# An encoder layer with two attention groups: the first modulation in half blocks, products of V ahead of the first unit, rope tables among the fillers, and denser steps of the second modulation

## The chip, the cores and the metric

The kernel runs on one core of one Trainium2 chip. The metric is device time in microseconds (us) of one execution, the median of several runs. A core has five instruction streams: TensorE (PE, with its weight loads as PEld), VectorE (DVE), ScalarE (ACT), GpSimd (POOL) and SyncE (SP), which here issues the DMAs. Each engine works through its own stream in order; semaphores tie the streams together.

## The reference, cut to what matters

One layer on a sequence of 1024 tokens of width 1024, all in float32. A conditioning vector c gives six vectors of 1024 (shift, scale and gate for the mixer and for the channel part):

```
mod = silu(c) @ w_ada + b_ada                    # w_ada: 1024 x 6144
sh_a, sc_a, g_a, sh_m, sc_m, g_m = split(mod, 6)
h    = rmsnorm(x, g_attn_norm) * (1 + sc_a) + sh_a
proj = h @ w_in                                  # q_lat, kv_lat, k_rope, ca_qkv
q, k, v of 8 latent heads: up-projections of the latents, rmsnorm, rope(q, positions), rope(k, positions)
o_mla = chunk-causal attention(q, k, v)          # 8 heads
cq, ck = rmsnorm per head of ca_qkv; cv
o_ca  = attention over a band of 9 chunks of 64, with relative bias     # 8 heads
x = x + g_a * (concat(o_mla, o_ca) @ w_out)
h = rmsnorm(x, g_mlp_norm) * (1 + sc_m) + sh_m
u = causal_dwconv(h @ w_up, width 3); x = x + g_m * ((silu(gate) * val) @ w_down)
```

rope needs sin and cos of position times frequency, for 1024 positions and 16 frequencies.

## The kernel before, in words

Products that need float32 are done as three products of a high and a low part (`gemm3`). Weights come as 256-column pieces (`load_w`: a DMA on SP, the high part on ScalarE, the low part on GpSimd).

**The start.** SP loads the packed vectors, the eight tiles of x (128 tokens by 1024, 512 KB each), the first 1 MB block of the modulation's weights (`adaw_0`), and the weights `wq0`. Each tile of x is squared and summed on ScalarE (line 212), its root on GpSimd (`rsqrt_mean`, line 116, an operation of power), and scaled on VectorE (line 214). Then a loop goes over the eight blocks d of 128 columns. In each block VectorE multiplies eight pieces of `adaw_d`, 256 wide (128 columns of scale and 128 of shift), by the conditioning vector's eight columns and adds them up (`adacc`, lines 241 and 243); two small matmuls (`p_ada`) sum over the partitions; VectorE makes the block's column of `modT` (lines 249 to 251). `mod_transpose` turns x into columns (four transposes on TensorE), applies `modT` twice on ScalarE (`hT`, the high part, line 224, and `hv`) and takes the low part on VectorE or GpSimd. 24 products with `wq0` follow (line 150), which build q and k of the first pair of heads for all 1024 tokens in PSUM (`qk0`).

Behind the loop `rope_tables` computes the sin and cos tables on VectorE (two Sin on ScalarE). Then `qk_norm` normalises q and k of the first pair: copy and square on ScalarE, a reduce on VectorE, the power and the multiply (line 373) on GpSimd. The buffers of the start are given back to the attention's pool at that place.

**The attention.** It consists of 32 units (16 of banded heads, 16 of latent heads; `ca_unit`, `mla_unit`), each of four tiles of 128 queries. `prep` transposes q and k to pages (`qk_page`, line 615). `Unit.scores` issues the products of scores (line 655), the minimum on VectorE (lines 670 and 674; the scores are negated), Exp on ScalarE (line 681), the high and low half-precision parts of the probabilities, and a transposing DMA on SP. `Unit.values`, three tiles later, multiplies by V (line 721).

**The fillers.** Between the tiles the program puts pieces of other work, from a list of generators: `v0` (`f_v(0)`, the products of V for the first two pairs, 192 matmuls in PSUM tiles `ipv0`), `qk1`, `qk2` (tiles `ipq`), `v1`, `qk3`, `m` (the latents, `f_m`, which need the rope tables), `up0`, `up1`, `oca`. `pace` issues as many pieces as a ratio of the costs of the scores and values asks for; `need` issues all pieces of the keys that a unit needs. Most filler keys also feed a side generator `f_ada`, which computes the gate of the mixer and the second modulation: per step two DMAs of 128 KB and two multiply-adds 256 wide on VectorE (`aacc`, lines 428 and 430), or a small matmul. One step is taken for every 2000 ns of filler cost; there are 73 steps.

```
            if key not in ("v0", "up0", "up1", "oca"):
                nside[0] += c
                while nside[0] > 2000:
                    nside[0] -= 2000
                    next(side[0], None)
```

**What sets the order.** A scheduler orders the instructions of each engine from the program by its own simulation of the times, within the dependences, with raised priority for scores, probabilities and values (`tc.high_priority`). `tc.issue_after(x)` holds an instruction behind instruction x in its engine's order. Buffers come from tagged pools: a tile waits until the tile that last had its buffer is done. Tag "A" (three buffers of 256) serves `adacc`, `aacc` and the pieces `aw`; tag "pg" has six buffers.

Behind the attention come the output projection and the MLP (from `load_wo(0, ...)` on), with a third modulation piece `gmbc` (lines 1008 and 1010, the same kind of multiply-add, 512 wide).

Of the kernel before, what the change touches and what calls it, by code (L numbers as in the profile page):

```python
# [23 lines left out]
P = 128  # L24
D = 1024
# [12 lines left out]
GSTEP, LAG = 2, 4  # L38
DEPTH = 3
# [19 lines left out]
def _grid(x, q):  # L59
    return round(x / q) * q  # L60


def layer_kernel(ctx, tc, I, out):
# [81 lines left out]

    def gemm3(pt, pairs, start=True, stop=True):

        n = len(pairs)
        for i, (sh, sl, mh, ml) in enumerate(pairs):
            pe.matmul(pt, sh, mh, start=(start and i == 0), stop=False)  # L150
            pe.matmul(pt, sh, ml, start=False, stop=False)  # L151
            pe.matmul(pt, sl, mh, start=False, stop=(stop and i == n - 1))  # L152
# [17 lines left out]
    def load_w(name, src, ncol, he="a", ssw=None):  # L170
        tiles = []
        for k in range(ND):
# [7 lines left out]
            for c0 in range(0, ncol, 256):  # L180
# [4 lines left out]
                if ssw is not None:  # L185
                    junk = qtile(f"{name}j{k}")
# [6 lines left out]

    xs = []
# [6 lines left out]
    wada = []  # L201

    def load_ada(d):
        w = st.tile([P, ND, 2, P], F32, name=f"adaw_{d}", tag="wa", bufs=2)
        sp.dma_start(w[:], I["w_ada_a"][d])
        wada.append(w)

    load_ada(0)
# [26 lines left out]
    qk0 = [ps.tile([P, 1024], F32, name=f"qk0_{i}", tag="S", bufs=2) for i in range(2)]  # L235
    for d in range(ND):
        if d + 1 < ND:
            load_ada(d + 1)
        w = wada[d]
        acc = apg.tile([P, 2, P], F32, name=f"adacc_{d}", tag="A", bufs=3)  # L240
        dve.tensor_scalar(acc[:], w[:, 0], cs[:, 0:1], None, op0=MUL)
        for k in range(1, ND):
            dve.scalar_tensor_tensor(acc[:], w[:, k], cs[:, k:k + 1], acc[:], op0=MUL, op1=ADD)
        pt = ps.tile([P, 512], F32, name=f"p_ada{d}", tag="mm", bufs=2)
        for i in range(2):
            pe.matmul(pt[:, i:i + 1], acc[:, i, :], ones[:, 0:1], start=True, stop=True)
# [15 lines left out]
    def rope_tables():  # L262
        sp.dma_start(pos_i[:], I["pos"])
        buf = [st.tile([P, 8, NT, 16], F32, name=f"rt{i}", tag="x", bufs=4) for i in range(8)]
        cnt = [0]

        def T():
            cnt[0] += 1
            return buf[(cnt[0] - 1) // 8][:, (cnt[0] - 1) % 8]

        def rnd(src, q):
            o = T()
            dve.tensor_scalar(o, src, q, MAGIC, op0=MUL, op1=ADD)
            dve.tensor_scalar(o, o, MAGIC, None, op0=SUB)
            return o

        def fma(n, c, b):
            o = T()
            dve.scalar_tensor_tensor(o, n, c, b, op0=MUL, op1=ADD)
            return o  # L280

        p1 = _grid(TWO_PI, 2.0 ** -9)
        p2 = _grid(TWO_PI - p1, 2.0 ** -21)
        p3 = TWO_PI - p1 - p2

        def reduce(src):
            n = rnd(src, 1.0 / TWO_PI)
            r = fma(n, -p1, src)
            r = fma(n, -p2, r)
            return fma(n, -p3, r)  # L290

        pf = cst.tile([P, NT], F32, name="pf")
        dve.tensor_copy(pf[:], pos_i[:])
        ang = T()
        dve.tensor_tensor(ang, pf[:].unsqueeze(2).to_broadcast([P, NT, 16]),
                          pk[:, C_INV:C_INV + 16].unsqueeze(1).to_broadcast([P, NT, 16]), op=MUL)
        nh = rnd(ang, 2.0 ** -20)
        rem = fma(nh, -(2.0 ** 20), ang)
        nm = rnd(rem, 2.0 ** -8)
        lo = fma(nm, -(2.0 ** 8), rem)  # L300
        tot = reduce(lo)
        for n, w in ((nh, 2.0 ** 20), (nm, 2.0 ** 8)):
            c = w - round(w / TWO_PI) * TWO_PI
            c1 = _grid(c, 2.0 ** -9)
            x = T()
# [1053 lines left out]
```

## Time and profile before

| | before |
|---|---|
| median of 3 runs | 1423.73 us (1421.95 to 1424.95) |
| profiled execution | 1423.74 us, of it 1422.0 us of span |
| mean granted TensorE clock | 0.936 |
| TensorE busy | 1247.1 us (88%), 6704 matmuls |
| VectorE busy | 1081.8 us (76%) |
| GpSimd busy | 686.6 us (48%) |
| ScalarE busy | 620.6 us (44%) |
| DMA | 190.64 MB, mean 134 GB/s |

How to read it: the span goes from the first to the last recorded instruction. Shares are of the span. A row of an engine in "busy tenths" cuts the span into 40 equal slices of 35.55 us and gives the busy share of each in tenths; PEclk is the clock granted to TensorE in tenths of full speed. A row of a group has line, engine, operation, output <- inputs, shapes and count, then total busy us and mean ns of one, then the engine's idle time just before them and what ended most of it. A row of the timeline begins with the start in us and the duration; behind it stands in brackets the wait ahead of it and what ended it. A row of the table of stretches has the stretch, its length, the busy us of the engines with their counts, the granted clock, the DMA share and GB/s.

### The profile page before, as it was taken

How to read it: one execution, taken by the hardware profiler on the slowest of the kernel's cores; microseconds unless marked ns; L12 is line 12 of the kernel's file. 1: busy time of each engine (PE TensorE's matmuls, PEld its weight loads, DVE VectorE, ACT ScalarE, POOL GpSimd, SP SyncE). 2: the span in 40 equal slices, each digit the busy share in tenths (PEclk: the TensorE clock that was granted, in tenths of full speed). 3: DMA queues.
4: the chain of work that ended last, by engine and by line, in shares of the span. 5: the costliest groups of instructions: out<-in, count | busy, mean ns of one | idle time of the engine just before them, and what ended most of it. 6: DMA issues, size and time to landing. Idle time of an engine off the chain costs nothing.

```text
span 1422.0 us, 19886 instructions
## 1 busy us (share of the span) xinstructions
PE 1247.1 (88%) x6704; PEld 1031.6 (73%) x6704; DVE 1081.8 (76%) x1891; ACT 620.6 (44%) x1150; POOL 686.6 (48%) x673
## 2 busy tenths in 40 slices
PE   3859989998877688886695999999999999999998
PEld 2759977987765567765574887877778777888886
DVE  6864877566689997684467789989888889688667
ACT  4453344334356554453255443343344443543331
POOL 5263545265555673334562675676667775200000
PEclk9979996999888889997896999999999999999999
DMA  8423557545441478778731233333323223894451
GB/s 289 134 74 79 119 111 146 139 107 119 104 94 41 88 163 159 161 148 224 275 126 30 90 111 126 125 122 116 111 84 102 97 96 112 309 356 126 126 163 59
DMA packets 229602, 190.64 MB, mean 134 GB/s; under 512 B 149366, under 2 KB 180218, under 8 KB 228476
## 3 DMA queue, kind: packets, MB, share of 16 engines
q1 hardware_dynamic: 229500, 189.38, 48.1%
q8 instruction: 52, 0.85, 0.2%
q14 instruction: 50, 0.41, 0.1%
HBM read 117.24 MB, written 37.49 MB: 109 GB/s over the span
## 4 chain that ended last, share of the span: by engine, by line
PE 20%; DVE 19%; POOL 5%; issue 5%; ACT 4%; DMA 3%; SPq 1%; DVEq 0%; POOLq 0%; ACTq 0%
DVE u L1024 5%; DVE u L1023 4%; PE dnA_P L1171 2%; PE dnA_P L1173 2%; PE dnA_P L1172 2%; ACT u L1022 2%; PE dnB_P L1173 1%; PE dnB_P L1171 1%; PE dnB_P L1172 1%; DVE gmbc L1010 1%; DVE u L1100 1%; DVE c L1095 1%; DMA adaw<-w_ada 1%; PE p L934 1%; PE p L932 1%
## 5 line engine op out<-in xcount | busy, mean ns | idle before, releaser
L75 ACT ACTIVATE dnP<-dnr 128x1024 fp32r<-128x1024 f32 x73 | 77.4, 1062 | 111.0 <-PE dnA_P L1173 46.4
L1145 DVE TENSOR_TENSOR dnP<-dnr,dnP 128x1024 fp32r<-128x1024 f32 x72 | 88.3, 1230 | 47.0 <-ACT dnP L75 46.4
L1023 DVE SCALAR_TENSOR_TENSOR u<-c,pk,u 128x1023 f32<-128x1023 f32 x44 | 81.8, 1901 | 46.2 <-ACT u L1022 44.8
L71 POOL TENSOR_SCALAR hlm<-Pm,rim 128x512 f16<-128x512 f32 (+3 forms) x96 | 67.2, 710 | 79.6 <-DVE rim L684 36.0
L1024 DVE SCALAR_TENSOR_TENSOR u<-c,pk,u 128x1022 f32<-128x1022 f32 x44 | 84.3, 1955 | 0.0
L71 POOL TENSOR_SCALAR hlc<-Pc,ric 128x640 f16<-128x640 f32 (+2 forms) x64 | 45.3, 710 | 78.8 <-DVE ric L684 31.5
L681 ACT ACTIVATE Pc<-sc,mc 128x640 f32<-128x640 f32 (+2 forms) x64 | 42.1, 659 | 85.9 <-DVE mc L670 64.3
L655 PE MATMUL sm<-mk,mq 96*128 96x512 f32 (+3 forms) x288 | 70.1, 372 | 10.2 <-ACT Pm L681 6.8
L430 DVE SCALAR_TENSOR_TENSOR aacc<-aw,cs,aacc 128x256 f32<-128x256 f32 x84 | 44.5, 529 | 43.1 <-DMA aw<-w_ada 42.4
L655 PE MATMUL sc<-k,q 64*128 64x512 f32 (+3 forms) x288 | 70.6, 374 | 6.4 <-ACT Pc L681 3.8
L721 PE MATMUL pvm<-PTm,vt 128*128 128x128 f16 x576 | 48.2, 235 | 30.0 <-DMA PTm<-hlm 25.7
L705 DVE SCALAR_TENSOR_TENSOR hlm<-Pm,rim,hlm 128x512 f16<-128x512 f32 (+3 forms) x96 | 68.3, 725 | 5.2 <-POOL hlm L71 4.9
L721 PEld LDWEIGHTS <-vt 128*128 128x128 f16 x576 | 39.6, 106 | 40.7 <-issue 38.9
L681 ACT ACTIVATE Pm<-sm,mm 128x128 f32<-128x128 f32 (+3 forms) x64 | 47.2, 737 | 46.6 <-DVE mm L674 23.1
L655 PEld LDWEIGHTS sm<-mk,mq 96*128 96x128 f32 x288 | 49.7, 200 | 19.9 <-ACT Pm L681 10.1
L655 PEld LDWEIGHTS sc<-k,q 64*128 64x128 f32 x288 | 48.1, 209 | 20.3 <-ACT Pc L681 5.2
L1022 ACT ACTIVATE u<-c,pk 128x1024 f32<-128x1024 f32 x44 | 52.2, 1234 | 16.7 <-DVE c L1095 9.3
L75 ACT ACTIVATE wc<-ws 128x512 fp32r<-128x512 f32 x22 | 13.9, 632 | 102.9 <-DVE ws L949 102.9
L150 PE MATMUL ipq<-wq_s,hT 128*128 128x256 f32 x192 | 57.2, 298 | 0.0
L705 DVE SCALAR_TENSOR_TENSOR hlc<-Pc,ric,hlc 128x640 f16<-128x640 f32 (+2 forms) x64 | 48.9, 769 | 9.3 <-POOL hlc L71 9.2
L151 PE MATMUL ipq<-wq_s,hT 128*128 128x256 f32 x192 | 55.8, 291 | 0.0
L152 PE MATMUL ipq<-wq_s,hT 128*128 128x256 f32 x192 | 55.0, 287 | 0.0
(404 smaller groups left out, 4464.9 us busy)
## 6 DMA issues: line engine op xcount, KB each, us to landing
wu<-w_up SPq DMA_DIRECT2D x44, 512.0 KB, 3.5
dnr<-g_d SPq DMA_DIRECT2D x73, 256.0 KB, 4.2
aw<-w_ada SPq DMA_DIRECT2D x96, 128.0 KB, 2.3
g_d<-u SPq DMA_DIRECT2D x22, 512.0 KB, 2.7
dnr<-w_down SPq DMA_DIRECT2D x44, 256.0 KB, 5.4
x<-x SPq DMA_DIRECT2D x16, 512.0 KB, 8.4
adaw<-w_ada_a SPq DMA_DIRECT2D x8, 1024.0 KB, 5.1
g_d<-gs SPq DMA_DIRECT2D x22, 256.0 KB, 2.1
```

Of the source, the lines that this page charges most:

```text
L71: pool.tensor_scalar(o, i, s, 1.0, op0=MUL, op1=MUL)
L75: act.activation(o, i, AF.Copy)
L150: pe.matmul(pt, sh, mh, start=(start and i == 0), stop=False)
L151: pe.matmul(pt, sh, ml, start=False, stop=False)
L655: last = pe.matmul(s[:, c:c + w], qpg[rs_, a, q], kpgs[kh][rs_, b, ko:ko + w], start=(a == 0 and b == 0), stop=(a == 1))
L681: act.activation(pr[:, :n], sv, AF.Exp, bias=m[:], scale=-1.0, accum_out=rsum[:, 0:1])
L705: dve.scalar_tensor_tensor(hl[:, w:2 * w], pp, ri[:], hl[:, :w], op0=MUL, op1=SUB)
L721: last = pe.matmul(u.pv[:, c], u.vst(j), mov, start=(x == 0), stop=(x == len(todo) - 1))
L1022: act.activation(u[:], c, AF.Identity, scale=pk[:, cv + 2:cv + 3], bias=pk[:, cv + 3:cv + 4])
L1023: dve.scalar_tensor_tensor(u[:, 1:], c[:, :S - 1], pk[:, cv + 1:cv + 2], u[:, 1:], op0=MUL, op1=ADD)
L1024: dve.scalar_tensor_tensor(u[:, 2:], c[:, :S - 2], pk[:, cv:cv + 1], u[:, 2:], op0=MUL, op1=ADD)
L1145: r = f(*a, **k)
```

## The change

- **First modulation in half blocks.** The weights are laid out on the host as four pairs of blocks, each `[128, 8, 512]`. A pair is loaded in four pieces of `[128, 2, 512]` (512 KB, tag "wa", five buffers in place of two of 1 MB). The four pieces of pair 0 are loaded ahead of x, and the positions ahead of them. VectorE makes one accumulator per pair with eight multiply-adds 512 wide (32 in all, where there were 64 of 256); pair dd+1 is issued at the first block of pair dd.
- **Products of V ahead of unit 0.** The weights `wv0` are loaded inside the loop at block 4, and 16 filler steps (`NPRE`) are issued before the first unit. The scale of V (`pow2_scale`) is issued behind the first tile's products instead of ahead of them. The transposes of `qk_page` are held behind the last of these products.
- **Normalisation of the first pair.** The multiply of `qk_norm` for `qk0` goes to VectorE.
- **Rope tables among the fillers.** `rope_tables` becomes a generator with 14 rotating and two kept slots in two "pg" tiles; it takes a step at each filler step of `qk1`, held behind the last minimum of the scores on VectorE. What is left of it is issued at the start of `f_m`. The two Sin stand next to each other in the program.
- **Denser second modulation.** One step per 1500 ns of filler. Its loads are held behind the last transposing DMA on SP, its multiply-adds behind the last minimum on VectorE.

```diff
+NPRE = 16
...
     def gemm3(pt, pairs, start=True, stop=True):
...
-            pe.matmul(pt, sl, mh, start=False, stop=(stop and i == n - 1))
+            last = pe.matmul(pt, sl, mh, start=False, stop=(stop and i == n - 1))
+        anchor["pe"] = last.ins
...
+    sp.dma_start(pos_i[:], I["pos"])
+    def load_ada(dd, c):
+        w = st.tile([P, 2, 512], F32, name=f"adaw_{dd}_{c}", tag="wa", bufs=5)
+        sp.dma_start(w[:], I["w_ada_a"][dd][:, 2 * c:2 * c + 2])
+        wada[dd, c] = w
+    for c in range(4):
+        load_ada(0, c)
     xs = []
...
+    def ada_pair(dd):
+        acc = rtile(f"adacc_{dd}")
+        for k in range(ND):
+            w = wada[dd, k // 2][:, k % 2]
+            if k == 0:
+                dve.tensor_scalar(acc[:], w, cs[:, 0:1], None, op0=MUL)
+            else:
+                dve.scalar_tensor_tensor(acc[:], w, cs[:, k:k + 1], acc[:], op0=MUL, op1=ADD)
+        accs[dd] = acc
+    ada_pair(0)
     for d in range(ND):
-        if d + 1 < ND:
-            load_ada(d + 1)
-        w = wada[d]
-        acc = apg.tile([P, 2, P], F32, name=f"adacc_{d}", tag="A", bufs=3)
-        dve.tensor_scalar(acc[:], w[:, 0], cs[:, 0:1], None, op0=MUL)
-        for k in range(1, ND):
-            dve.scalar_tensor_tensor(acc[:], w[:, k], cs[:, k:k + 1], acc[:], op0=MUL, op1=ADD)
+        dd, half = divmod(d, 2)
+        if half == 0 and dd + 1 < ND // 2:
+            for c in range(4):
+                load_ada(dd + 1, c)
+            ada_pair(dd + 1)
+        if d == 4:
+            wv0 = load_w("wv0_", I["w_v"][0], 256, ssw=ssw0,
+                         jt=lambda n: st.tile([P, 512], F32, name=n, tag="hv", bufs=2))
...
-    rope_tables()
     startp.__exit__(None, None, None)
...
-    def qk_norm(src_psum, nm, qn, j0):
+    def qk_norm(src_psum, nm, qn, j0, eng=pool):
...
-        pool.tensor_tensor(qn[...
+        eng.tensor_tensor(qn[...
...
     def f_v(pp):
...
             yield from proj2(pt, t, w, 256)
+            if t == 0:
+                vscale["c", pp] = pow2_scale(f"c{pp}", ssw[:], hb[:], ND, 2.0 * D)
+                sc = vscale["c", pp][0]
...
     def f_ada():
...
+                    with tc.issue_after(anchor["sp"]):
+                        sp.dma_start(w[:], I["w_ada"][k * P:(k + 1) * P, c0:c0 + 256])
+                    with tc.issue_after(anchor["dve"]):
...
     def f_m():
+        for _ in rope[0]:
+            pass
...
+    def rope_tables():
+        buf = [pgtile([P, 8, NT, 16], F32, f"rt{i}") for i in range(2)]
+        def T():
+            n = cnt[0] % 14
...
+        dve.tensor_scalar(cl2, (yield from reduce(c2)), pi_s, -pi_s, op0=MIN, op1=MAX)
+        act.activation(sn, cl, AF.Sin)
+        act.activation(cn, cl2, AF.Sin)
+        yield
...
     def qk_page(src, name, rows, tag, bufs, gain):
-        for j in range(4):
-            pe.transpose(pt[:rows, j * P:(j + 1) * P], src(j), ident[:])
+        with tc.issue_after(first[0]):
+            for j in range(4):
+                pe.transpose(pt[:rows, j * P:(j + 1) * P], src(j), ident[:])
...
+                    anchor["dve"] = dve.tensor_tensor_reduce(...).ins     # likewise the tensor_reduce of latent heads
+                    anchor["sp"] = sp.dma_start_transpose(tt[:, :2 * w // P, :], hl[:, :2 * w]).ins
...
+            if key == "qk1":
+                if rope[0] is None:
+                    rope[0] = rope_tables()
+                with tc.issue_after(anchor["dve"]):
+                    next(rope[0], None)
             if key not in ("v0", "up0", "up1", "oca"):
                 nside[0] += c
-                while nside[0] > 2000:
-                    nside[0] -= 2000
+                while nside[0] > 1500:
+                    nside[0] -= 1500
                     next(side[0], None)
...
+    for _ in range(NPRE):
+        fill_step()
+    first = [anchor["pe"]]
```

More of the change, by code (lines that the diff above doesn't have):

```diff
@@ L395, in f_v @@
     def f_v(pp):
-        ssw = cst.tile([P, ND], F32, name=f"ssw{pp}")
-        w = load_w(f"wv{pp}_", I["w_v"][pp], 256, ssw=ssw)
-        vscale["c", pp] = pow2_scale(f"c{pp}", ssw[:], hb[:], ND, 2.0 * D)
-        sc = vscale["c", pp][0]
+        ssw = cst.tile([P, ND], F32, name=f"ssw{pp}") if pp else ssw0
+        w = load_w(f"wv{pp}_", I["w_v"][pp], 256, ssw=ssw) if pp else wv0
         for t in range(0, NT, 2):
@@ L507, in layer_kernel @@
+    rope = [None]
     G = {}
```

158 lines of the change are left out of this document (79 added, 79 removed).

## The prediction

> **What bounds the kernel now.** I read the page first, for the engine that is busiest over the span and for the place where it is not.
>
> ```profile
> PE 1247.1 (88%) x6704; PEld 1031.6 (73%) x6704; DVE 1081.8 (76%) x1891; ACT 620.6 (44%) x1150; POOL 686.6 (48%) x673
> PE   3859989998877688886695999999999999999998
> PEclk9979996999888889997896999999999999999999
> ```
>
> TensorE is busy 88% of the 1422.0 us, so a gain must come from its idle slices. Four stretches are weak: the first three slices, slice 6 (a clock of 6 tenths), slices 10 to 15, and slice 19. The change edits only code ahead of the end of attention (slice 18 and earlier), so I cut that part into stages with the table of stretches.
>
> ```profile
> 0.00:28.90 28.90, 4.80 (x12) 2.38 (x12) 15.79 (x34) 13.85 (x26) 14.16 (x30) 1.00 0.82 297
> 28.90:77.30 48.40, 41.90 (x276) 37.52 (x276) 43.61 (x104) 25.09 (x40) 15.16 (x13) 0.96 0.43 144
> 77.30:101.30 24.00, 9.34 (x57) 8.41 (x57) 17.23 (x53) 11.05 (x34) 19.74 (x23) 0.64 0.22 66
> 101.30:200.00 98.70, 96.85 (x768) 87.61 (x768) 60.57 (x178) 40.06 (x94) 43.07 (x55) 1.00 0.45 100
> 213.00:240.00 27.00, 23.92 (x114) 20.16 (x113) 20.03 (x60) 13.49 (x36) 18.16 (x22) 0.50 0.73 149
> 350.00:450.00 100.00, 76.71 (x412) 61.61 (x412) 77.54 (x239) 49.67 (x131) 51.83 (x77) 0.83 0.40 88
> ```
>
> Columns: stretch, length, then busy us of PE, PEld, DVE, ACT, POOL, the granted clock, the DMA share, GB/s. Up to 101.3 us TensorE works 56.0 us and idles 45.3 us. Behind that it is the bound (96.85 of 98.70 us). So the start is a chain of waits, and what it saves is worth its full size as long as TensorE stays the bound behind it. The ends of the three start stages are these rows:
>
> ```profile
> 28.08 0.78 ACT L224 ACTIVATE hT<-ht_ps,modT 128x512 fp32r<-128x512 f32 x1 [3.73 <-DVE modT L250]
> 28.91 0.58 PE L150 MATMUL qk<-wq_s,hT 128*128 128x256 f32 x1 [3.19 <-ACT hT L224]
> 83.46 0.69 PE L615 MATMUL q_ps<-ident,qn 128*128 128x128 f32 x2 [6.17 <-POOL qn L373]
> 89.06 0.69 PE L615 MATMUL q_ps<-ident,qn 128*128 128x128 f32 x2 [4.91 <-POOL qn L373]
> 101.30 0.49 PE L655 MATMUL sc<-k,q 64*128 64x128 f32 x2
> ```
>
> The first product of the modulated block waits for the modulation on VectorE (modT); the first transposes of q wait for GpSimd's normalisation; the first score comes at 101.30 us.
>
> **Part 1: first modulation in half blocks, its weights ahead of x.** The order of x and the multiply-adds today:
>
> ```profile
> 4.92 1.06 ACT L212 ACTIVATE xj<-x 128x1024 bf16<-128x1024 f32 x1 [1.53 <-DMA x<-x]
> 15.26 1.06 ACT L212 ACTIVATE xj<-x 128x1024 bf16<-128x1024 f32 x1
> 18.45 0.75 DVE L214 TENSOR_SCALAR x<-x,rx 128x1024 f32<-128x1024 f32 x1 [0.71 <-POOL rx L116]
> L241 DVE TENSOR_SCALAR adacc<-adaw,cs 128x256 f32<-128x256 f32 x8 | 6.2, 776 | 1.6 <-DMA adaw<-w_ada_a 1.5
> L243 DVE SCALAR_TENSOR_TENSOR adacc<-adaw,cs,adacc 128x256 f32<-128x256 f32 x56 | 32.3, 582 | 1.1
> L1010 DVE SCALAR_TENSOR_TENSOR gmbc<-adaw,cs,gmbc x14: 739/1223/1831, 865.0 to 992.7; 128x512 f32<-128x512 f32 x14
> L1008 DVE TENSOR_SCALAR gmbc<-adaw,cs x2: 475/476/476, 842.1 to 842.5; 128x512 f32<-128x512 f32 x2
> ```
>
> The eight loads of x are used every (15.26-4.92)/7 = 1.48 us. Four loads of the same 512 KB now stand ahead of them, so x comes 4 x 1.48 = 5.9 us later: the last x is scaled at 18.45+0.75+5.9 = 25.1 us, the fourth 4 x 1.48 earlier, at 19.2. The modulation of blocks 0 and 1 is done by then (four chunks from about 4.9 us on, eight multiply-adds behind). So the first modulated half block no longer waits for modT but for x: transposes and ScalarE put its first product at about 21, and the weights wq0, now loaded behind x, at about 22.5 (my allowance of 1.5), against 28.91.
>
> VectorE spends 6.2+32.3 = 38.5 us on 64 instructions 256 wide. After, there are 32 instructions 512 wide. The nearest rows are the same operations in the MLP: 739 ns undisturbed (the least), 1223 in the middle, beside GpSimd. That gives 4 x 0.48 + 28 x 0.74 = 22.6 us, or 36.2 at the median. I take near the lower, since GpSimd is idle two thirds of this stage (15.16 of 48.4). Three quarters of it follow x: 25.1 + 17 = 42 us, or 52 at the median. In the built order of the changed kernel the last modulation products (p_ada6, p_ada7) stand behind four of eight blocks on TensorE, which TensorE reaches at about 22.5 + half of 36 = 40. So the stage changes from bound by VectorE to bound by TensorE.
>
> **Part 2: products of V ahead of unit 0, normalisation on VectorE.** In the built order 150 of the 192 products of V (wv0) stand ahead of the first score, against 46 now, interleaved with blocks 4 to 7. Their price:
>
> ```profile
> 101.30:131.00 29.70, 20.50 (x147) 18.18 (x146) 3.84 (x8) 3.74 (x8) 1.00 0.37 84
> 28.90:77.30 48.40, 32.47 (x192) 27.60 (x192) 1.09 (x2) 0.96 0.43 144
> ```
>
> The first row is the table restricted to ipv (tile of V), the second restricted to qk: 20.50/147 = 0.139 us each, and 32.47/192 = 0.169 with the half-speed stretches in it. TensorE's work up to the first score after the change is then qk 32.47, transposes and modulation 41.90-32.47 = 9.4, V 150 x 0.139 = 20.9, pages of q and k 2 x 0.69: 64 us. With qk at 0.139 it is 58. From 22.5 the first score comes at 80.5 to 86.6 us; I take 83, 18.3 earlier. The chain of normalisation (ScalarE, VectorE, GpSimd's power, then the multiply, now on VectorE) lies beside V's products: in the built order 62 of them or of the last qk stand between the end of unit 0's first half and the transposes of q, 62 x 0.139 = 8.6 us, against 83.46-77.3 = 6.2 us of chain in the rows above. Moreover 104 more products of V are done by then, 104 x 0.139 = 14.5 us, which TensorE need not do behind 101.3, where it is the bound. **Credit: 18.3 + 14.5 = 32.8 us**, between 14.7+14.5 = 29 and 20.8+14.5 = 35.
>
> **Part 3: the rope tables among the fillers.** They leave the start and enter the stretch in which TensorE is busy all the time.
>
> ```profile
> 60.00:100.00 40.00, 14.71 (x49) 0.60 (x2) 0.74 0.20 59
> 60.00:100.00 40.00, 0.00 (x0) 0.00 (x0) 5.91 (x9) 0.74 0.20 59
> L681 ACT ACT_TABLE_LOAD x1 | 1.3, 1283 | 0.0
> 103.93 1.28 ACT L681 ACT_TABLE_LOAD   x1
> 105.23 0.37 ACT L681 ACTIVATE Pc<-sc,mc 128x128 f32<-128x128 f32 x1
> ```
>
> The first row is the tables (rt), DVE 14.71 us; the second the first group of the second modulation (aacc), 5.91 us, which was done early too and is now pinned behind the first minima of the scores. VectorE has 98.7-60.57 = 38 us free up to 200 us, so 20.6 more fit; but VectorE runs in order, and an exponential's minimum can queue behind two or three of these. Bounds: nothing, or all 20.6; I charge 4, near the free end because TensorE has fillers to run meanwhile. The built order also shows what the diff does not: the two Sin now fall between Exp, and four more table loads are on ScalarE (7 against 3). Each is 1.283 us, with Exp queued behind it: 5.1 us in all, ScalarE being 40% busy there. Bounds 0 and 5.1; I charge 2.5.
> The Trainium skill, "ScalarE: Activation LUTs", section on what ACT_TABLE_LOAD costs, gives 1283 ns for the load and some 1380 ns of drain, 2.66 us a switch. That would be 10.6 us for the four, and at the same half 5.3 instead of 2.5. The row agrees on the load; of a drain it shows nothing (load at 103.93, next activation at 105.23).
>
> **Part 4: second modulation in denser steps.** Its 73 steps (f_ada) come every 1500 ns of filler instead of every 2000. Each issues loads on SP, pinned behind the last transpose of probabilities there, and multiply-adds on VectorE, which wait for those loads in order, with minima of scores queued behind them. Today:
>
> ```profile
> 350.00:400.00 50.00, 1.17 (x8) 1.20 (x8) 8.15 (x16) 0.84 0.51 111
> 400.00:450.00 50.00, 0.00 (x0) 0.00 (x0) 3.81 (x7) 0.82 0.29 65
> ```
>
> (Third figure: VectorE on aacc.) Between 350 and 450 us TensorE idles 100 - 76.71 = 23.3 us, and these 8.15+3.81 = 12 us share VectorE with the minima. At three quarters of the spacing they end before 350, where fillers cover them. Gain between 0 (they lie beside a wait for transposes anyhow) and 12; I take 2, because VectorE is not full there (77.54 of 100). The half-clock stretch 213 to 240 us in the table of stretches could vanish too, since fillers (ipq2) now follow into scores that ran without any: at half clock 23.92 us of work, so up to 12 gained. I take 0, since denser loads pull the other way.
>
> **The sum.** -32.8 + 4 + 2.5 - 2 = -28.3 us. The profiled execution took 1423.74 us (1422.0 of span and 1.7 around it), which is the median of the three runs, 1423.73, to 0.01. Forecast: 1423.7 - 28.3 = **1395 us**. What is unknown moves it as follows: the credit 29 to 35, the tables and Sin 0 to 25.7, the denser steps 0 to 12 gained, the half clock 0 to 12 gained or as much lost.
>
> **Rivals.** *First, the loads bind the modulation.* Its weights now go through five buffers of 512 KB.
>
> ```profile
> adaw<-w_ada_a SPq DMA_DIRECT2D x8, 1024.0 KB, 5.1
> ```
>
> These 8.4 MB, x (8 x 512 KB, 4.2 MB) and wq0 (1.0 MB) make 13.6 MB. At the first stage's 297 GB/s, 7.5 are there by 25.1 us; at the second stage's 144 GB/s the other 6.1 take 42 us, to 67. Two of eight blocks (41.90/4 = 10.5 us), the normalisation (6.2) and the way from the second transposes to the first score (101.30-89.06 = 12.2) follow: first score at 96, a credit of 5.3+14.5 = 19.8 instead of 32.8, total **1408**. Against it: the DMA engines are 43% busy in that stage, so 144 is what was asked for, not what they give. Chance 0.13.
>
> *Second, given back.* VectorE and ScalarE charge in full for what enters a TensorE-bound stretch: 20.6+5.1 = 25.7 instead of 6.5, without the 2: 1423.7-32.8+25.7 = **1417**. For it: ScalarE's four loads are each ahead of an Exp that the row of Pc needs. Against it: VectorE has 38 us free there. Chance 0.16.
>
> *Third, slower: half-clock spells.* At 213 to 240 us TensorE is 89% busy at a clock of 0.50: a short lapse in its feed is enough to keep it there for 27 us, which costs 23.92/2 = 12 us. Ahead of it, fillers run dry:
>
> ```profile
> 200.00:213.00 13.00, 10.62 (x70) 8.37 (x69) 10.87 (x33) 7.09 (x20) 5.04 (x7) 0.87 0.53 123
> ```
>
> The denser steps make such lapses likelier: a multiply-add waits on VectorE for its load (42.4 us of idle time are put down to that in the row below), the load is pinned behind a transpose on SP, the minimum behind it is late, so is Exp, and TensorE's sequence of scores stops. 150 products of V taken ahead are also 104 fillers fewer to bridge it with.
>
> ```profile
> L430 DVE SCALAR_TENSOR_TENSOR aacc<-aw,cs,aacc 128x256 f32<-128x256 f32 x84 | 44.5, 529 | 43.1 <-DMA aw<-w_ada 42.4
> ```
>
> Two spells more leave a gain of 28.3-24 = 4; from the third on it is slower: **1431** (1395+36). Against it: from 101 to 200 us, with the same waits, the clock is 1.00. Chance 0.16, with 0.03 for a case in which the sides cancel.
> The Trainium skill, "TensorE: Matmul & The Clock Gate", section "Part 1: The HAM clock gate", has the half clock set in after an idle window of about 3.4 us and end after about 3.4 us of sustained work; by it a spell costs some 1.7 us, an estimate, and three cost 5 in place of 36, which leaves 1400. The row of 27 us at 0.50, with TensorE 89% busy, disagrees.
>
> **How the numbers follow.** The forecast has 0.52: its own range is 1383 (credit 35, nothing charged, 6 of the 24 that may be gained) to 1403 (credit 29, 10 charged, 2 gained). Loads 0.13, given back 0.16, cancelling 0.03, spells 0.16. The range takes in the first three cases down to 1376 (as 1383, with 7 more of the half-clock stretch's 12) and up to 1417: it leaves out the spells and little else, 0.2. A difference of 0.2%, 2.8 us, is about what a measurement of this kernel can tell from no change. Faster: 0.52+0.13+0.16 = 0.81; same 0.03; slower 0.16.
>
> **What the profile after would show.** Right: first modulated product near 22.5 instead of 28.91, VectorE's modulation at some 23 to 36 us in 32 rows, first score near 83 (80.5 to 86.6), four more ACT_TABLE_LOAD between Exp rows, TensorE still above 95% busy for the 100 us behind the first score, aacc over before 350. Wrong: adaw's loads as the releaser of the modulation, first score at 96 (the first rival); TensorE's idle time behind 83 released by Exp or minima that stand behind rt (the second); tenths of 5 in the clock's slices that were 9 (the third). What would make the forecast wrong altogether is a first score that comes early and a time of attention that grows by as much, as then TensorE would not have been the bound behind 101 us.

## The result, and the profile after

The changed kernel is slower: 1432.88 us median of six runs (1430.53 to 1441.81) against 1425.64 us of six runs of the kernel before, a ratio of 1.0056 with a 95% interval of 1.0035 to 1.0077. Forecast was 1395. The profiled execution took 1439.27 us, above its own median, while that of before lies 1.9 us below its median, so the two pages differ by 15.5 us of span where the medians differ by 7.2. The readings below are for direction and place, the medians for size. The granted clock shows by how much the page overstates: the profiled execution has 0.915, the lowest of the changed kernel's six, whose mean is 0.924, while the page of before has 0.936 and the 102 runs of before beside the experiments have 0.933 in the mean.

The page's busy times and slices of the changed kernel:

```profile
PE 1278.0 (89%) x6704; PEld 1059.2 (74%) x6704; DVE 1078.3 (75%) x1863; ACT 626.1 (44%) x1154; POOL 683.9 (48%) x669
PE   4898989999887879896694999999999999999998
PEclk9797977899787879998796999999999999999999
```

The first line holds the answer in short. TensorE does the same 6704 matmuls, but is busy 1278.0 us with them instead of 1247.1, 30.9 more. Its idle time (span less busy) fell from 174.9 to 159.5 us. So the change did what it says, 15.4 us of idle time are gone, and twice as much came back as slower matmuls. The row of the clock shows where, with the slices counted from 1 (the prediction counts them from 0): slices 2, 4 and 6 fell from 9 to 7, slices 3 and 7 rose (7 to 9, 6 to 7), and slices 11 to 15, all at 8 before, hold three sevens.

The table of stretches, the same stretches as before:

```profile
0.00:28.90 28.90, 8.46 (x29) 6.07 (x30) 16.13 (x29) 14.65 (x26) 14.66 (x28) 1.00 0.91 341
28.90:77.30 48.40, 42.85 (x282) 40.89 (x282) 31.24 (x63) 27.79 (x62) 27.19 (x28) 0.82 0.42 134
77.30:101.30 24.00, 22.82 (x181) 21.61 (x179) 12.43 (x27) 13.49 (x28) 11.97 (x14) 1.00 0.05 14
101.30:200.00 98.70, 88.59 (x611) 76.38 (x609) 72.34 (x237) 40.91 (x87) 40.18 (x50) 0.84 0.54 115
213.00:240.00 27.00, 23.51 (x164) 19.91 (x163) 18.24 (x57) 9.55 (x28) 10.15 (x12) 0.82 0.71 142
350.00:450.00 100.00, 81.28 (x415) 65.07 (x413) 68.06 (x212) 47.23 (x130) 46.18 (x80) 0.80 0.33 73
```

Third row: the wait for the normalisation is gone, TensorE is busy 22.82 of 24 us with products of V, where it was busy 9.34. Fourth row: the stretch that was full before (96.85 of 98.70 at a clock of 1.00) holds 611 matmuls in place of 768, at 0.84. The work that the start gained is lost within the next 100 us. Behind the last product with V (678.5 us, before 662.7) the two kernels take the same time, 759.0 and 759.3 us, so the whole difference arises ahead of it.

The rows that answer to the ends of the stages (timeline of the changed kernel), and behind them the group of the multiply-adds:

```profile
20.21 0.78 ACT L230 ACTIVATE hT<-ht_ps,modT 128x512 fp32r<-128x512 f32 x1 [0.59 <-PE ht_ps L227]
23.63 1.02 ACT L76 ACTIVATE wq_s<-wq_r 128x256 fp32r<-128x256 f32 x3
24.10 1.33 PE L227 MATMUL ht_ps<-ident,x 128*128 128x128 f32 x5 [0.99 <-DVE x L220]
25.08 0.56 PE L153 MATMUL qk<-wq_s,hT 128*128 128x256 f32 x1
54.76 1.48 PE L268 MATMUL p_ada<-ones,adacc 128*128 128x1 f32 x8 [2.02 <-DVE adacc L252]
86.63 0.38 PE L656 MATMUL q_ps<-ident,qn 128*128 128x128 f32 x2
95.69 0.49 PE L696 MATMUL sc<-k,q 64*128 64x128 f32 x2
```
```profile
L252 DVE SCALAR_TENSOR_TENSOR adacc<-adaw,cs,adacc 128x512 f32<-128x512 f32 x28 | 25.3, 903 | 0.7
```

ScalarE makes the first high part hT of the modulated block at 20.21, but that of wq0, whose load now lies behind x, only at 23.63; and TensorE's order has transposes of the other half ahead of the first product, which wait for x until 24.10. So the first product comes at 25.08. Ahead of the transposes of q (86.63) there is no wait left. The first score comes at 95.69, 5.6 us earlier than before instead of 18.

What one loss looks like, from the timeline of TensorE and a table of stretches of the changed kernel, and the same stretch before (last line):

```profile
128.97 0.69 PE L656 MATMUL q_ps<-ident,qn 128*128 128x128 f32 x2 [2.30 <-POOL qn L328]
137.53 1.23 PE L762 MATMUL pvc<-PTc,v 128*128 128x128 f16 x10 [2.51 <-DMA PTc<-hlc]
```
```profile
120.00:126.80 6.80, 5.96 (x48) 4.68 (x48) 3.45 (x7) 1.90 (x4) 2.31 (x4) 1.00 0.58 135
126.80:147.40 20.60, 15.49 (x64) 12.72 (x65) 18.64 (x65) 8.55 (x15) 5.40 (x6) 0.50 0.41 86
```
```profile
126.80:147.40 20.60, 20.60 (x166) 19.62 (x165) 7.29 (x19) 9.13 (x19) 9.71 (x13) 1.00 0.29 80
```

By the records of the clock it falls to 0.50 at 126.9 us, 0.2 us into the stop of 2.30 us (ahead of it, from 123.5 us on, shorter waits leave TensorE 73% busy), and stays there for 20.5 us. In them TensorE begins 64 matmuls; before, it began 166. The idle time itself is 5 us; the slow work costs half of 15.49 more.

### The profile page after: what moved, and what is told of

It is laid out like the page before. It is cut to its first block, busy times and chain, and to the rows that moved or that the text cites. A ratio compares the mean times of both kernels' runs of the same rounds, so it can differ in the third digit from the quotient of the medians.

```text
span 1437.5 us, 19909 instructions
## 1 busy us (share of the span) xinstructions
PE 1278.0 (89%) x6704; PEld 1059.2 (74%) x6704; DVE 1078.3 (75%) x1863; ACT 626.1 (44%) x1154; POOL 683.9 (48%) x669
## 4 chain that ended last, share of the span: by engine, by line
DVE 26%; PE 23%; issue 7%; POOL 6%; ACT 5%; DMA 5%; SPq 0%; DVEq 0%; POOLq 0%; ACTq 0%
DVE u L1073 5%; DVE u L1072 4%; DMA PTm<-hlm 2%; PE dnA_P L1220 2%; PE dnA_P L1221 2%; PE dnA_P L1222 2%; DMA wor<-w_out 2%; ACT u L1071 2%; DVE hlm L746 1%; PE dnB_P L1221 1%; PE dnB_P L1222 1%; PE dnB_P L1220 1%; PE sm L696 1%; DVE u L1149 1%; DVE mm L715 1%
## 5 line engine op out<-in xcount | busy, mean ns | idle before, releaser
L76 ACT ACTIVATE dnP<-dnr 128x1024 fp32r<-128x1024 f32 x73 | 77.3, 1061 | 110.9 <-PE dnA_P L1222 46.4
L696 PE MATMUL sc<-k,q 64*128 64x256 f32 (+3 forms) x288 | 74.4, 389 | 9.7 <-ACT Pc L722 4.5
L696 PE MATMUL sm<-mk,mq 96*128 96x512 f32 (+3 forms) x288 | 75.4, 396 | 8.2 <-ACT Pm L722 7.5
L696 PEld LDWEIGHTS sm<-mk,mq 96*128 96x128 f32 x288 | 53.4, 215 | 20.6 <-ACT Pm L722 13.8
L153 PE MATMUL ipq<-wq_s,hT 128*128 128x256 f32 x192 | 62.1, 323 | 0.0
L762 PE MATMUL pvc<-PTc,v 128*128 128x128 f16 x480 | 50.8, 241 | 10.5 <-DMA PTc<-hlc 5.9
L154 PE MATMUL ipq<-wq_s,hT 128*128 128x256 f32 x192 | 60.2, 314 | 0.0
L155 PE MATMUL ipq<-wq_s,hT 128*128 128x256 f32 x192 | 59.5, 310 | 0.0
```

The source lines that it names most:

```text
L76: act.activation(o, i, AF.Copy)
L696: last = pe.matmul(s[:, c:c + w], qpg[rs_, a, q], kpgs[kh][rs_, b, ko:ko + w], start=(a == 0 and b == 0), stop=(a == 1))
L762: last = pe.matmul(u.pv[:, c], u.vst(j), mov, start=(x == 0), stop=(x == len(todo) - 1))
```

## The experiments

Each kernel was timed over several rounds beside the kernel before. The first table gives the medians and the ratios with their intervals, and span, busy and idle time of TensorE from the first part of each page. A page is one execution, up to 6.4 us off its kernel's median (e5 below, the changed kernel above).

| run | what it is | median us | ratio to before | span | busy | idle |
|---|---|---|---|---|---|---|
| before | | 1425.6 to 1427.4 | | 1422.0 | 1247.1 | 174.9 |
| changed | all parts | 1432.9 | 1.0056 [1.0035, 1.0077] | 1437.5 | 1278.0 | 159.5 |
| e1 | changed, tables at the start | 1429.2 | 1.0018 [1.0004, 1.0033] | 1423.4 | 1256.9 | 166.5 |
| e2 | changed, steps at 2000 ns | 1466.1 | 1.0281 [1.0263, 1.0299] | 1461.4 | 1263.4 | 198.0 |
| e3 | changed, no steps ahead | 1430.4 | 1.0022 [1.0007, 1.0037] | 1428.9 | 1262.2 | 166.7 |
| e4 | start alone | 1426.3 | 0.9995 [0.9982, 1.0009] | 1420.8 | 1254.8 | 166.0 |
| e5 | modulation alone | 1416.0 | 0.9933 [0.9919, 0.9947] | 1407.7 | 1246.2 | 161.5 |
| e6 | V and multiply alone | 1416.3 | 0.9939 [0.9918, 0.9960] | 1412.2 | 1242.9 | 169.3 |
| e7 | e5, multiply on VectorE | 1430.6 | 1.0031 [1.0020, 1.0043] | 1426.6 | 1258.5 | 168.1 |
| e8 | e4, more fillers | 1421.9 | 0.9965 [0.9948, 0.9983] | 1424.9 | 1255.3 | 169.6 |
| e9 | before, one stop | 1440.5 | 1.0108 [1.0090, 1.0127] | 1438.7 | 1255.7 | 183.0 |
| e10 | before, four stops | 1451.1 | 1.0182 [1.0163, 1.0201] | 1449.5 | 1263.7 | 185.8 |
| e11 | e4, multiply on GpSimd | 1417.5 | 0.9937 [0.9921, 0.9953] | 1410.7 | 1247.6 | 163.1 |
| e12 | changed, multiply on GpSimd | 1425.5 | 1.0001 [0.9985, 1.0016] | 1423.4 | 1254.2 | 169.2 |
| e13 | e11 and tables among fillers | 1419.9 | 0.9954 [0.9933, 0.9975] | 1417.4 | 1250.6 | 166.8 |
| e14 | e11 and held, denser steps | 1431.5 | 1.0039 [1.0018, 1.0059] | 1429.8 | 1259.6 | 170.2 |
| e15 | e12 and an unused multiply on VectorE | 1416.2 | 0.9927 [0.9909, 0.9946] | 1411.0 | 1242.9 | 168.1 |
| e16 | changed and an unused multiply on GpSimd | 1433.6 | 1.0049 [1.0032, 1.0067] | 1430.6 | 1262.0 | 168.6 |
| e17 | e11, more fillers | 1422.4 | 0.9962 [0.9947, 0.9976] | 1416.7 | 1247.2 | 169.5 |
| e18 | e6, multiply on GpSimd | 1424.1 | 0.9977 [0.9960, 0.9993] | 1426.3 | 1255.5 | 170.8 |

Every variant that keeps part of the change, but e2, has 4 to 15 us less idle time than before. What separates 1416 from 1433 is mainly the busy column: e5, e6, e11 and e15 (1416 to 1418) are at 1243 to 1248, the changed kernel, e3, e7, e14 and e16 (over 1430) at 1259 to 1278. The clock, which is on record for every run and not for the profiled one alone, goes the same way: a mean of 0.933 to 0.938 for each of the former, of 0.924 to 0.930 for each of the latter.

**Undoing one part (e1 to e4).** My theory was crowding (tables, Sin loads and second modulation cause the stops), the rivals cover and scatter. (The expectation of e4 takes TensorE's idle time up to 100 us in the changed kernel as 24.9 us; its table of stretches has 27.2.)

e1, the old `rope_tables()` ahead of `startp.__exit__`, and no step at `key == "qk1"`:

> The changed kernel with one part undone: the rope tables are computed at their old place behind the first modulation, none of them among the fillers. Crowding (my theory: the half-clock spells between 100 and 260 us come from short stops of TensorE, and the stops from what the change puts on VectorE and ScalarE there, tables and Sin loads ahead of minima and Exp): the loss to half clock up to 350 us falls from 40.6 towards the 19.9 of before, idle time up to 100 us rises by 5 to 10, total 1417 to 1425. Cover (rival: 104 products of V used up ahead of unit 0 leave too few fillers to bridge the stops): loss to half clock as in the changed kernel, total 1433 to 1440. Scatter (rival: any other order of the instructions moves the spells, and no part is to blame): total within 10 us of 1433 either way, with spells at other places.

e2:

```diff
-                while nside[0] > 1500:
-                    nside[0] -= 1500
+                while nside[0] > 2000:
+                    nside[0] -= 2000
```

> The changed kernel with the steps of the second modulation at 2000 ns of filler again instead of 1500, its holds kept. Crowding: VectorE gets a quarter fewer multiply-adds per time up to 350 us, so loss to half clock there falls by 5 to 10, total 1423 to 1429. Cover: total 1431 to 1435. Scatter: within 10 us of 1433, spells at other places.

e3 (`NPRE = 0`, and `qk_page` without its hold):

> The changed kernel without the 16 filler steps ahead of the first unit and without the hold on the transposes of q and k. Cover: the loss to half clock between 100 and 260 us goes back to about half, total 1420 to 1427. Crowding: loss to half clock stays; the wait for the normalisation has no products of V beside it, idle time up to 100 us rises by 5 to 12, total 1437 to 1445. Scatter: between 1425 and 1445, spells at other places.

e4 (e1, with 2000 ns and without the holds in `f_ada`):

> The start alone: half-block modulation, products of V ahead of unit 0, the multiply of the first normalisation on VectorE; rope tables at their old place, second modulation at 2000 ns and without its holds. Crowding: idle time up to 100 us near the 24.9 of the changed kernel plus at most 10, loss to half clock near that of before, total 1408 to 1418. Cover: loss to half clock as in the changed kernel, total 1433 to 1440. Scatter: anything from 1415 to 1440.

e1 gave 3.7 us of the 7 back, e3 2.4. Both times lie outside what crowding and cover had promised and inside the wide ranges of scatter. In e3 the products of V began just as early (at 56.3 us by the timeline, against 56.7), so it did not test the cover. e2 missed them all: 33 us slower than the changed kernel. Its timeline of TensorE shows the larger part of the reason:

```profile
709.61 1.01 PE L401 MATMUL p_ada<-ones,aacc 128*128 128x1 f32 x4 [22.71 <-DVE aacc L388]
722.45 1.01 PE L401 MATMUL p_ada<-ones,aacc 128*128 128x1 f32 x4 [11.83 <-DVE aacc L388]
```

I read this so: with the holds, steps that have not been taken by the end of the fillers cannot be moved up, and 34.5 us of waits stand behind the attention. Part of them replaces other waits: from the last product with V on, e2 takes 774.8 us and the changed kernel 759.0, 15.8 of the 23.9 by which their spans differ. The denser steps are what the holds need, not a saving. And e4, the start alone, stands level with before: crowding had promised 1408 to 1418 there, cover 1433 to 1440. So my first theory fell as the main cause.

**One part alone (e5 to e8).** e5 is the kernel before with the half-block modulation only; e6 the old modulation with V and the multiply of e4; e7 is e5 with `qk_norm(..., dve)`; e8 is e4 with `R_CA = 2.1`.

> The kernel before with the half-block modulation alone (its weights and the positions ahead of x, five buffers, 32 multiply-adds 512 wide); products of V, normalisation, tables and second modulation as before. Lost cover (my theory now: the start's gain is real, but the products of V taken ahead leave the first units without work between their scores, and the short stops that follow put TensorE on half clock): first score at 88 to 93 us, the 100 us behind it at full clock as before, total 1415 to 1420. Absorbed (rival: whatever is saved ahead of the first score is waited for later, since the band units up to 430 us are bound by their own chain of minima, Exp, transposes and not by TensorE): first score as early, but the first score of the latent heads at 430 to 434 us again, total 1424 to 1428.

> The kernel before with products of V ahead of unit 0 and the multiply of the first normalisation on VectorE, and the old modulation (1 MB blocks, 64 multiply-adds 256 wide). Lost cover: idle time up to 100 us falls by 8 to 12, and idle time and half clock between 100 and 200 us, 1.7 us in all before, rise by 12 to 20: total 1425 to 1433. Absorbed: the same early gain, given back later than 200 us, total 1424 to 1428.

> As e5, with the multiply of the first normalisation on VectorE as well. Lost cover: the first score another 1 to 2 us earlier than in e5, total 1413 to 1419. Absorbed: 1424 to 1428.

> The start alone (e4) with 2.1 in place of 1.9 as the ratio of filler cost to the cost of band scores and values, so that more fillers stand between the first tiles. Lost cover: idle time and half clock between 100 and 200 us, 13.9 us in e4, fall to under 8, total 1416 to 1423. Absorbed: 1424 to 1429, with what is won up to 200 us lost behind it.

Each early saving does reach the end: e5 is 9.9 us faster than before, e6 9.6. So the saving is not absorbed by a chain of the band units. But together (e4) they give nothing, and e7, with nothing but four multiplies of 128 by 512 on the other engine, is 14.6 us above e5. Lost cover had promised e6 to be slower and e7 to be faster: that theory fell too. e7 has 6.6 us more idle and 12.3 us more busy time than e5, in the same 6704 matmuls. e8 is 4.4 us below e4 and in lost cover's range, but not by its mechanism: idle time and half clock between 100 and 200 us are 10.3 us in it, not under 8.

**A stop by itself (e9, e10).** In the kernel before, ahead of a tile's scores (abridged):

```diff
+            if n in STOPS:                      # (10,) or (6, 10, 14, 18)
+                    pool.tensor_scalar(w[:], ones[:, 0:8], lastrs[0][:, 0:1], 1.0, op0=MUL, op1=MUL)
+                    for _ in range(2):
+                        pool.tensor_tensor(w[:], w[:], nhalf[:].to_broadcast([P, 8]), op=ALU.pow)
+                    x = pe.matmul(pt[:, 0:8], ones[:], w[:], start=True, stop=True)
+                with tc.issue_after(x.ins):
+                    pace(u.scores(i), R_CA if u.band else R_MLA)
```

> The kernel before with one stop put into TensorE's clean stretch (97 to 209 us at full clock): ahead of the eleventh tile's scores TensorE does one small matmul that waits for two chained powers on GpSimd, which start from that tile's predecessor's Exp; what follows in the program is held behind it. Nothing of the result changes. Spells (a stop of 1 to 3 us is followed by about 10 us of half clock, and both are lost for good): total 4 to 8 us above the kernel before, a spell within 5 us of the stop. Absorbed (the band units are bound by their own chain, and later waits shrink by what was lost): 0 to 2 us above it. Only the stop counts (the half clock costs nothing, since TensorE waits later anyway): 1 to 3 us above it.

> The same with four stops, ahead of tiles 7, 11, 15 and 19. Spells: 15 to 30 us above the kernel before, with three or four spells between 120 and 209 us. Absorbed: 0 to 4 us. Only the stops count: 4 to 12 us.

The timeline of TensorE in e9 and its table of stretches:

```profile
153.13 1.23 PE L723 MATMUL pvc<-PTc,v 128*128 128x128 f16 x10 [8.04 <-DMA PTc<-hlc]
157.33 0.54 PE L838 MATMUL stp<-stop,ones 128*128 128x8 f32 x2
```
```profile
125.00:145.00 20.00, 20.00 (x168) 18.94 (x167) 5.46 (x11) 8.27 (x17) 8.63 (x11) 1.00 0.31 81
153.10:164.60 11.50, 10.20 (x50) 9.01 (x50) 3.64 (x13) 2.37 (x5) 3.84 (x4) 0.50 0.19 37
```

The stop came out longer than meant: TensorE waited 8.04 us for transposed probabilities ahead of the inserted matmul (line 838). Behind it the clock is 0.50, with TensorE busy 10.20 of 11.50 us. By the medians the one stop costs 13.2 us at the end of the program, 23.7 the four, so "absorbed" falls. In the pages, idle and busy time of e9 are 8.1 and 8.6 us above those of before, those of e10 10.9 and 16.6, so not idle time alone is lost. That 8.04 of stop plus half of 10.20 gives 13.1 is luck in part: up to 260 us e9 loses less to half clock than before does (10.9 us against 13.7), and its lag behind before is 22.2 us at the first score of the latent heads (450.6 against 428.4) and 14.6 at the last product with V. And both runs have another order of instructions, and one changed word moved the time by up to 14.6 us in the pairs of this case; only the 23.7 of the four stops is above that.

**The multiply's engine (e11, e12), the other parts on the better start (e13, e14).** e11 and e12 change one word, `dve` to `pool`, in e4 and in the changed kernel.

> The start alone (e4) with the multiply of the first normalisation on GpSimd as before: half-block modulation and products of V ahead of unit 0 together. If it was that multiply on VectorE which cost the 10 us that each part gains alone (e7 against e5, 14.6 us): total 1403 to 1412. If the two early gains do not add, since what they save is the same idle time and the stops that follow are more (e4): 1418 to 1428.

> The changed kernel with the multiply of the first normalisation on GpSimd as before and nothing else undone. If that multiply on VectorE is what cost: 1417 to 1423. If tables, Sin loads and held steps between 100 and 260 us cost: 1429 to 1436.

> e11 (half-block modulation, products of V ahead, multiply on GpSimd; 1417.5) with the rope tables among the fillers, second modulation as before. If the tables and the four Sin loads cost: 1422 to 1427, with more loss between 100 and 260 us. If only the held and denser second modulation costs: 1415 to 1420.

> e11 with the second modulation held behind the last transpose and minimum and stepped at 1500 ns, rope tables at their old place. If this costs: 1422 to 1427, with stops released by the second modulation's multiply-adds (aacc). If only the tables cost: 1415 to 1420.

Three pairs now said that the multiply on VectorE costs (14.6 us in e5 and e7, 8.8 in e11 and e4, 7.4 in e12 and the changed kernel), though e11 and e12 fell short of what that theory had promised (at most 1412 and 1423). The tables among the fillers cost 2.4 us on e11 (e13, within the two intervals) and 3.7 on e1 (the changed kernel), but gain 6.0 on e14 (e12 is e14 with the tables among the fillers): their sign stays open. The held and denser steps cost 14.0 on e11 (e14), 5.6 on e13 (e12), 2.9 on e4 (e1): a cost each time, of no fixed size.

**Is it the engine, or the order? (e15, e16).** A multiply whose result nothing reads is added on the other engine, into the buffer of the squares:

```diff
+        if nm[0] == "0":
+            (dve if eng is pool else pool).tensor_tensor(sq[:]..., raw[:]..., r[:]..., op=MUL)
```

> e12 (the changed kernel with the multiply on GpSimd; 1425.5) with a second, unused multiply of the same size on VectorE, written into the square's buffer. If VectorE's load or place at the start costs: 1430 to 1436, as the changed kernel. If only what waits for the multiply matters: 1424 to 1428. If the planner's order behind it decides (scatter): anywhere from 1415 to 1440, and not ordered by engine.

> The changed kernel (multiply on VectorE; 1432.9) with a second, unused multiply on GpSimd. If the multiply on VectorE costs by itself: 1430 to 1436. If the planner's order decides (scatter): anywhere from 1415 to 1440.

e15 does more work than e12, on VectorE, and is 9.3 us faster. The pages' first part of e12 and e15:

```profile
PE 1254.2 (88%) x6704; PEld 1038.6 (73%) x6704; DVE 1078.0 (76%) x1859; ACT 623.9 (44%) x1154; POOL 697.6 (49%) x673
```
```profile
PE 1242.9 (88%) x6704; PEld 1030.2 (73%) x6704; DVE 1076.8 (76%) x1863; ACT 625.6 (44%) x1154; POOL 690.6 (49%) x673
```

The gain is 11.3 us of TensorE's busy time in the same matmuls; idle time differs by 1.1. (The page of e15 is 3.4 us below its median; over all runs the mean clock is 0.928 in e12 and 0.936 in e15.) VectorE's four more instructions are there (1863 against 1859). The tables of stretches of e12 and e15:

```profile
101.30:350.00 248.70, 225.01 (x1557) 195.24 (x1556) 178.04 (x540) 100.68 (x264) 117.84 (x163) 0.90 0.55 124
350.00:660.00 310.00, 250.86 (x1592) 204.95 (x1590) 247.91 (x683) 154.92 (x358) 152.44 (x199) 0.87 0.58 115
```
```profile
101.30:350.00 248.70, 226.06 (x1603) 198.69 (x1602) 180.65 (x557) 106.00 (x277) 115.31 (x169) 0.92 0.57 129
350.00:660.00 310.00, 242.74 (x1575) 197.03 (x1575) 242.31 (x666) 154.72 (x351) 152.69 (x198) 0.89 0.58 123
```

The clock is 0.02 higher in both. In the traces another matmul stands at 1645 of TensorE's 6704 places, from the 417th on. That fits scatter and no theory of the engine. e16, level with the changed kernel, decides nothing: both readings allowed it.

**Putting gains together (e17, e18).**

> e11 (1417.5) with 2.1 in place of 1.9 as the ratio of filler cost, which gave 4 us on e4 (e8). If the gains add: 1410 to 1415. If they are the same stops: 1416 to 1420.

> e6 (the old modulation with products of V ahead, 1416.3) with the multiply on GpSimd. If the multiply on VectorE costs by itself, as in three pairs: 1404 to 1410. If the planner's order decides: 1412 to 1428.

They do not add, and e17 met neither of its ranges: it is 4.8 us above e11, though the same ratio gave 4.4 on e4. e18, with the multiply on GpSimd, is 7.9 us above e6: the sign of the three pairs turned round. The versions whose intervals lie below before and the changed kernel are e5, e6, e8, e11, e13, e15, e17 and e18, at 0.9927 to 0.9977 of before; which of the four fastest, e5, e6, e11 and e15, is best, the intervals do not tell.

## Why the prediction was wrong

**The step that failed** is that what the start saves is worth its full size at the end, with TensorE as the bound at full clock behind it and the half clock taken at 0. Between 101.3 and 200 us TensorE was busy 88.59 of 98.70 us at 0.84, where it had been 96.85 at 1.00. What half clock takes, counted as half of TensorE's busy time in the records of half clock, is 96.4 us over the whole page; before, it was 60.3. These 36.1 us more, less 15.4 of idle time and 5.2 by which the busy time weighted by the clock is smaller, are the 15.5 by which the spans differ. By the clocks of all runs (0.924 and 0.933) the part of the half clock is smaller than on these two pages, in keeping with the medians.

- **The credit of 32.8 us: mis-sized, 20.1 came in the sum's own terms.** The first score stood behind 150 products of V, as read in the built order, so the 14.5 for 104 of them came; but it came at 95.69 and not at 83, so 5.6 of the 18.3 came. The sum let TensorE run from 22.5 without a stop and at full clock. The trace has the first product at 25.08 (2.6 late), 7.8 us of idle time from there to the first score, and 7.9 lost to half clock (0.82 between 28.9 and 77.3); the work itself was 5.5 shorter than planned. VectorE stayed the bound of the modulation, busy 29.61 of 30.92 us from 25.08 on: the last accumulators came at 54.7, forecast 42, and TensorE stopped for `adacc` ahead of blocks 2 and 6 (the 2.02 us of the last is shown above). The 28 multiply-adds took 903 ns each in the mean, between the rows of 739 and 1223 that bounded them. Loads did not bind: VectorE waited for `adaw` once, 3.4 us ahead of the first accumulator, so the first rival is out; that its first score, 96, is nearly the measured one is luck. The cover of the normalisation by products of V was right. By another measure, TensorE's busy time weighted by the clock up to 100 us, the gain is 14.4 us (64.9 against 50.5).
- **Rope tables and Sin loads, 6.5 us charged: not shown, not even in sign.** The three pairs have 3.7, 2.4 and -6.0 us. The order with four more table loads came as read: ScalarE's timeline shows them in and just behind the slow stretch above:

```profile
139.34 1.28 ACT L532 ACT_TABLE_LOAD   x1
146.13 1.28 ACT L722 ACT_TABLE_LOAD   x1 [0.57 <-DVE mc L711]
148.32 1.28 ACT L533 ACT_TABLE_LOAD   x1
149.95 1.28 ACT L722 ACT_TABLE_LOAD   x1
```

- **Denser steps, 2 us gained: wrong in sign.** Three pairs have 2.9 to 14.0 us of cost for steps and holds together, and e2 shows that the holds make density necessary. The half-clock stretch at 213 to 240, taken at 0, did improve (164 matmuls at 0.82 instead of 114 at 0.50); what it gained was lost at other places.
- **What the sum lacked was a term for the half clock.** It moved idle time as if the rest kept its speed. The third rival had the mechanism: half-clock spells, forecast 1431, measured 1432.9. That the number agrees so well is luck: it priced three spells at 12 us each on top of a forecast that gained 28, and on the page five more begin between 100 and 660 us (16 against 11), most of them shorter than the 27 us that the price was read from, and a start that gained less. Its place was only partly right, too. It blamed the multiply-adds of the second modulation; the trace has them among the releasers, as in the row below, but it is also the transposes of probabilities, Exp and the next unit's pages, and e4 and e7 lose as well without a denser second modulation.

```profile
309.38 0.58 PE L401 MATMUL p_ada<-ones,aacc 128*128 128x1 f32 x4 [2.65 <-DVE aacc L388]
```

- **The row weighed against the Trainium skill** ("TensorE: Matmul & The Clock Gate", "Part 1: The HAM clock gate"): half clock after an idle window of about 3.4 us, and back after as long of work. The spells that begin between 100 and 660 us in the traces' records of the clock last 3.4, 6.8, 10.2, 13.7, 17.1, 20.5, 23.9 or 30.7 us, multiples of that window, which agrees. That a spell ends after any busy window does not: the one at 126.8 lasted 20.5 us with TensorE three quarters busy. Nor need the window ahead of a spell be idle: TensorE was 73% busy in that one, and the counts in the last section show the same.

That idle time and half clock together set the time is shown by the accounts of busy and idle time. That added stops cost more than their own length is borne out by e9 and e10, of which only e10 is above what one changed word did here. That an instruction nobody reads can move the time by 9.3 us, through TensorE's clock, is shown by e15 against e12; that it does so through the planner's order is argued, as the reading left over: idle time and weighted busy time of the two agree to 1.1 and 0.3 us, but the order and the unused instruction came together. Which single change of order makes or spares a given stop stays open: no two variants here differ in one place alone.

## What to carry to other kernels

Where TensorE is the bound, count its losses in two columns, idle time and the same matmuls' longer busy time: a change can win the first and lose twice as much in the second. A start that is shortened in a kernel ordered by a planner comes with another order for all that follows, here worth 9 us for an unused instruction and up to 15 for one changed word, so a forecast of a few per cent needs that spread in its range, and one timed variant says little about the edit that it is named for. Run a neutral variant beside it (an unused instruction of the same size) before an effect is put down to the edit.

## What the hardware showed that was not expected

As far as counts show, the half clock goes by how full a window of 3.4 us was, and needs no long stop. In all twenty traces each record of the clock, but for the last, which the end of the trace cuts, is a whole multiple of 3.41 us long, so the records give the windows. Counted from 100 to 660 us, with TensorE at full clock: all 110 windows in which it was busy less than 40% were followed by half clock, 151 of 364 between 40 and 70%, 17 of 327 between 70 and 85%, and 2 of 1761 above. At half clock, none of 233 windows under 80% was followed by full clock, 18 of 86 between 80 and 95%, and 251 of 379 above. So a kernel that is 75% busy can stay at half clock for long, and where a stop falls in its window is part of its price.

Counted by stops from full clock: of 461 of 0.3 to 0.8 us 102 were followed by a spell within 5 us of their start, of 335 between 0.8 and 1.5 us 136, of 152 between 1.5 and 2.2 us 108, and of 105 longer ones 98. But stops come in groups. Of those that stand alone (no other of 0.3 us or more from 7 us before to 5 us after) it is 2 of 89, 7 of 61, 28 of 49 and 25 of 28: a short stop alone is seldom enough, one of 1.5 us often is. A count of what follows is not yet a cause; e9 and e10 are the places where stops were put in. The spells last 7.5 to 11.0 us in the mean of a trace. In all twenty traces TensorE's busy time weighted by the clock is 1180 to 1188 us; the span is that, plus idle time, plus the 58 to 96 us that the half clock takes.
